# Expert weights of an MoE layer: the later loads as pairs of 4 MiB in a ring of five places

## The chip, the cores and the metric

The kernel runs as one program on one core of a Trainium2 chip. The metric is the time of one execution in microseconds (us); lower is better. TensorE (PE) multiplies matrices, with its weight loads shown as PEld; VectorE (DVE), ScalarE (ACT) and GpSimd (POOL) work on elements; the queue of SyncE (SP) issues nearly all transfers from the memory outside the core (HBM) into the core's SBUF, which has 128 partitions. 16 DMA engines carry those transfers.

## The reference

256 tokens of width 1024 pass through two blocks of attention and feed-forward layers, and then through a second model's block that ends in a mixture of experts. Each token takes the best 4 of 32 experts; only chosen pairs count:

```python
vals, idx = lax.top_k(logits, TOP_K)
gate = jax.nn.softmax(vals, axis=-1)
...
up = jnp.dot(xb, w_up[eb]) + b_up[eb]
glu, lin = jnp.split(up, 2, axis=-1)
glu = jnp.minimum(glu, SWIGLU_LIMIT)
lin = jnp.clip(lin, -SWIGLU_LIMIT, SWIGLU_LIMIT)
act = glu * jax.nn.sigmoid(SWIGLU_ALPHA * glu) * (lin + 1.0)
return jnp.dot(act, w_down[eb]) + b_down[eb]
```

All is float32. The weights of one expert are 1024 x 2048 up and 1024 x 1024 down, 12 MiB; the 32 experts' are 384 MiB, and every expert's weights are read once.

## The kernel before

The first half of the time goes to the attention and feed-forward layers, whose weights come in chunks of 1 MiB (rows of 8 KB, lines 304 and 307). The change doesn't touch them. The MoE layer follows (`moe`).

**Chunks.** On the host, `_expert_chunks` cuts each expert's weights into `PARTS` = 6 chunks of 2 MiB, each [128 partitions x `WIDE` = 4096 floats], so a partition's row is 16 KB. Chunks 0 and 1 hold the gate half of the up weights, 2 and 3 the linear half, 4 and 5 the down weights.

**Units.** The experts are sorted by how many tokens chose them, and take steps of a fixed pattern, `KINDS = "FFFM" + 4 * "MLDLMLL"`. A step of kind L has one unit of 32 token slots, F and M one unit of 64, and D, the busiest experts, two units of 64 slots that use the same six chunks one after the other. For each unit PE runs, in a fixed order, the gate half (chunks 0 and 1), then the down product of the unit before (that one's chunks 4 and 5), then the linear half (chunks 2 and 3). With a D step the chunks 0 and 1 stay in use until its second unit has passed them, which is after the first unit's chunks 2 and 3. All products of tokens and weights are recorded at line 1839 (`products`); the tile of their results is `sc`, the chunks' tile is `ring`. Between the products stand gathers of tokens (line 1804), the outputs' sums (1904) and other small matmuls.

**Loads.** The order of first use makes a list of 192 loads (`seq`), numbered here from 0. D steps after the change's point are the loads 76, 77 (its chunks 0 and 1), 80, 81 (2 and 3), 82, 83 (4 and 5); 118, 119, 122, 123, 124, 125; and 160, 161, 164, 165, 166, 167. Load k goes into place k mod 11 of a ring of `RING` = 11 places, each a pool of one tile of 16 KB in each partition (176 KB in all). The SP queue issues the loads in this order, with line 2019 or 2016. Each issue waits until PE has read the place's old chunk for the last time, and until the transfer issued eight before it has landed, since eight completion semaphores are used in turn. The last chunk comes in three pieces, so that PE can start on it sooner.

```python
t = ring[nd[0] % RING].tile([P, WIDE], F32, tag="ring", name="ring")
...
nc.sync.dma_start(t[:, f], src[bass.ds(row, P), f])
```

After the last unit two places of the ring serve for a row of gains (`post`) and for the result (`res`), and the output leaves in four transfers. `overflow` holds a path for experts with more tokens than their slots, which runs only then.

Of the kernel before, what the change touches and what calls it, by code (L numbers as in the profile page):

```python
# [9 lines left out]
F32 = mybir.dt.float32  # L10
# [9 lines left out]
P = 128  # L20
S = 256
D = 1024
# [11 lines left out]
NE = 32  # L34
# [4 lines left out]
WIDE = 2 * CHUNK  # L39
PARTS = 6  # L40
RING = 11

SLOTS = (0, 8, 1, 6, 7, 5, 2, 9, 10, 3, 4)

WB = (8, 0, 2, 8)
TAKEN = 1000.0
# [86 lines left out]
def _consts2():  # L133
# [26 lines left out]
FIXED = (0, 11, 22)  # L160
# [4 lines left out]
UNITS = [(s, o, n) for s in range(NE)  # L165
         for o, n in {"D": ((0, CAP), (CAP, CAP)), "L": ((0, CAP // 2),)}.get(KINDS[s], ((0, CAP),))]
NU = len(UNITS)
# [37 lines left out]
def _expert_chunks(up, down):  # L205


    u = up.reshape(NE, 2, 4, P, 2, D).transpose(0, 4, 1, 3, 2, 5).reshape(NE, 4, P, WIDE)
    d = down.reshape(NE, 2, 2, 2, P, D).transpose(0, 2, 4, 3, 1, 5).reshape(NE, 2, P, WIDE)
    return np.concatenate([u, d], 1).reshape(NE * PARTS, P, WIDE)  # L210


def _pack(pieces):
# [32 lines left out]
def quads(t):  # L246

    return t.rearrange("p (a b) -> p a b", a=4)
# [86 lines left out]
class Kernel:  # L335
# [1603 lines left out]
    def more_slots(self, ring, positions):  # L1939

        nc, v, tc = self.nc, self.nc.vector, self.tc
        src = self.ins["experts"].rearrange("n p c -> (n p) c")
        with tc.tile_pool(name="ovs", bufs=1) as sp_, tc.tile_pool(name="ovf", bufs=1) as ep:
            at = sp_.tile([P, 1], F32, name="at")
            v.memset(at, 0.0)
            with tc.For_i(0, NE) as e:
                hot = ep.tile([P, NE], F32, tag="hot", name="hot")
                junk = ep.tile([P, NE], F32, tag="junk", name="junk")
                pos = ep.tile([P, 2, 1], F32, tag="opos", name="opos")
                gate = ep.tile([P, 2, 1], F32, tag="ogate", name="ogate")  # L1950
                bsel = ep.tile([96, 1], F32, tag="obsel", name="obsel")
                v.tensor_scalar(hot, self.iota, at, None, ALU.is_equal)
                for t in range(2):
                    for a, b in ((positions, pos), (self.gate, gate)):
                        v.scalar_tensor_tensor(junk, a[:, t], 1.0, hot, ALU.mult, ALU.mult, accum_out=b[:, t])
                v.scalar_tensor_tensor(junk[0:96], self.bsel[0:96], 1.0, hot[0:96], ALU.mult, ALU.mult, accum_out=bsel)
                sel = self.select(bsel, ep)
                for r in range(2):
                    raw = {}

                    def chunk(c):
                        if c not in raw:
                            raw[c] = ring[c].tile([P, WIDE], F32, tag="ring", name="oring")
                            nc.sync.dma_start(raw[c], src[bass.ds((e * PARTS + c) * P, P)])
                        return raw[c]

                    xg = ep.tile([P, KD, CAP], F32, tag="yh", name="oxg")
                    pr = self.pick([(pos[:, :, 0], r * CAP, CAP)])
                    for j in range(0, KD, 2):
                        self.gather(xg, j, pr, self.pt())  # L1970
                    sp, gs = self.spread(pos[:, :, 0], r * CAP, CAP, gate[:, :, 0], ep, 1)
                    gl = self.expert_gate(self.expert_up(0, xg, sel, chunk), ep, "gl", "yl")
                    a = self.expert_turn(self.expert_act(self.expert_up(1, xg, sel, chunk), gl, ep), ep)
                    self.expert_out(self.expert_down(a, sel, gs, chunk, ep, "yh", "yl"), sp)
                v.tensor_scalar(at, at, 1.0, None, ALU.add)

    def moe(self):
        nc, v, tc, ins = self.nc, self.nc.vector, self.tc, self.ins
        ctx = ExitStack()
        ring = [ctx.enter_context(tc.tile_pool(name=f"ring{i}", bufs=1, reuse_waits="tile", side="right"))  # L1980
                for i in range(RING)]
        ring = [ring[i] for i in SLOTS]
        mp = ctx.enter_context(tc.tile_pool(name="moe", bufs=1, reuse_waits="tile"))
        raw, nd = {}, [0]
        src = ins["experts"].rearrange("n p c -> (n p) c")
        which = [None] * NE
# [10 lines left out]
        seq = list(dict.fromkeys(uses))  # L1997
        place = {n: i for i, n in enumerate(seq)}

        spare = [ring[(len(seq) + i) % RING] for i in range(2)]  # L2000

        def load(upto):
            while nd[0] < min(upto, len(seq)):
                e, c = n = seq[nd[0]]
                t = ring[nd[0] % RING].tile([P, WIDE], F32, tag="ring", name="ring")
                row = c * P
                cols = [slice(0, WIDE)]
                if nd[0] == len(seq) - 1:
                    cols = [slice(0, 2 * D), slice(2 * D, 3 * D), slice(3 * D, WIDE)]
                if e >= len(FIXED):  # L2010
                    if which[e] is None:
                        which[e] = nc.values_load(self.order[0:1, e:e + 1], engines=(mybir.EngineType.SP,), min_val=0,
                                                  max_val=NE - 1)
                    row = which[e] * (PARTS * P) + row
                    for f in cols:
                        nc.sync.dma_start(t[:, f], src[bass.ds(row, P), f])
                else:
                    row += FIXED[e] * PARTS * P
                    tc.keep_in_program_order(nc.sync.dma_start(t, src[row:row + P]))
                raw[n] = t  # L2020
                nd[0] += 1

        def chunks(u):
            e = UNITS[u][0]

            def chunk(c):

                load(place[e, c] + (RING if u + 1 == NU or UNITS[u + 1][0] != e else 1))
                return raw[e, c]
            return chunk  # L2030

        load(RING)
        gp = self.gp = ctx.enter_context(tc.tile_pool(name="grp", bufs=1, reuse_waits="tile"))
        groups, spreads = {}, {}
# [26 lines left out]
        def post():  # L2061

            col = self.tiny.tile([P, KD], F32, tag="gcol", name="gcol2", bufs=1)
            v.tensor_tensor(col, self.modc[:, 40:48], self.g2[:, 3], ALU.mult)
            t = spare[0].tile([P, WIDE], F32, tag="ring", name="post")
            self.post_row, r = t[:, 0:D], t[:, D:2 * D].rearrange("p (a b) -> p a b", a=KD)
            v.tensor_tensor(r, self.ones.unsqueeze(1).to_broadcast([P, KD, P]), col.unsqueeze(2).to_broadcast([P, KD, P]),
                            ALU.mult)

            def half(h):  # L2070
                ps = self.pt()
                for i in range(4):
                    nc.tensor.transpose(ps[:, i * P:(i + 1) * P], r[:, 4 * h + i], self.ident)
                nc.scalar.copy(self.post_row[:, h * 512:h * 512 + 512], ps)

            return [lambda h=h: half(h) for h in range(2)]
# [10 lines left out]
        for u, (e, _, _) in enumerate(UNITS):  # L2087
            n = {}
# [39 lines left out]

        def finish():

            res = spare[1].tile([P, WIDE], F32, tag="ring", name="res")[:, 0:2 * D].rearrange("p (t d) -> p t d", t=2)
            s4 = self.tiny.tile([P, 4, 2], F32, tag="ss", name="s4", bufs=1)[:, 0:2]
            half = lambda h: slice(h * 512, h * 512 + 512)
            for t in range(2):
                for h in range(2):
                    nc.scalar.activation(self.sc(), self.out[t][h], AF.Square, accum_out=s4[:, t, h:h + 1])
                for h in (1, 0):
                    v.tensor_tensor(res[:, t, half(h)], self.out[t][h], self.post_row[:, half(h)], ALU.mult)
            r = self.natural_rstd(s4)
            for t in range(2):  # L2140
                for h in range(2):
                    a = res[:, t, half(h)]
                    v.scalar_tensor_tensor(quads(a), quads(a), r[:, t:t + 1], self.x[:, 4 * h:4 * h + 4, t * P:(t + 1) * P],
                                           ALU.mult, ALU.add)
                    nc.sync.dma_start(self.outs["out"][t, :, half(h)], a)

        finish()
        self.overflow([p for p in ring if p not in spare], finish)
        ctx.close()


# [181 lines left out]
```

## Time and profile before

| | us |
|---|---|
| Median of 3 runs | 2136.68 |
| Lowest, highest | 2136.51, 2139.9 |
| The profiled execution: its time | 2137.93 |
| The profiled execution: its span | 2136.2 |
| PE busy in the span | 2010.3 (94%) |
| DVE, ACT busy | 1169.9 (55%), 798.1 (37%) |
| Loads of experts' chunks: 191 of 2048 KB and 3 pieces | 30.4 from issue to landing (median) |

The profile's span runs from the first instruction to the last; the execution's own time is 1.7 us longer. Of the page's 40 slices of 53 us each, those from the 23rd on are the MoE layer.

### The profile page before, as it was taken

The numbers are of one execution on the slowest core, as the hardware profiler recorded it, in microseconds if no ns is written. First come the engines' busy times: TensorE is split into PE (matmuls) and PEld (weight loads), VectorE is DVE, ScalarE is ACT, GpSimd is POOL, SyncE is SP. The second block draws the span as 40 slices with busy tenths as digits, with TensorE's granted clock in tenths as the row PEclk, the third lists the DMA queues.
The fourth block names the chain that finished last, engine by engine and source line by source line (L and its number), as shares of the span: only waits on it lengthen the run. The fifth ranks groups of instructions, "written<-read, shape, count | busy, mean of one in ns | idle before, by whom it ended". The sixth has DMA issues, their size and how long they took to land.

```text
span 2136.2 us, 34339 instructions
## 1 busy us (share of the span) xinstructions
PE 2010.3 (94%) x13872; PEld 1376.2 (64%) x13872; DVE 1169.9 (55%) x2572; ACT 798.1 (37%) x1541; POOL 97.0 (5%) x147
## 2 busy tenths in 40 slices
PE   8999999999999999999999999999789878978895
PEld 6888888888888888888887633444334333433342
DVE  7888878986999887996787522222112111211112
ACT  7655556654554455655576211111101111101111
POOL 1001001221000101000100000000000000000000
PEclk9999999999999999999999999999999999999998
DMA  7555426876765533775535999999999999999996
GB/s 264 200 185 185 156 89 210 303 278 220 251 243 190 196 109 119 258 255 202 187 119 195 391 428 427 406 401 427 428 426 427 427 427 427 426 427 427 428 426 277
DMA packets 66164, 633.89 MB, mean 297 GB/s; under 512 B 10048, under 2 KB 11200, under 8 KB 15312
## 3 DMA queue, kind: packets, MB, share of 16 engines
q1 hardware_dynamic: 59568, 619.62, 73.6%
q0 software_dynamic: 2288, 7.28, 1.0%
q10 hardware_dynamic: 4144, 4.74, 0.7%
q8 instruction: 111, 1.82, 0.3%
q14 instruction: 53, 0.43, 0.1%
HBM read 626.10 MB, written 5.51 MB: 296 GB/s over the span
## 4 chain that ended last, share of the span: by engine, by line
PE 68%; DMA 24%; DVE 5%; ACT 1%; issue 1%; POOL 0%; ACTq 0%; SPq 0%; DVEq 0%; POOLq 0%
DMA ring<-in_experts_dram 22%; PE sc L1839 16%; PE acc L372 14%; PE acc L371 7%; PE sc L372 7%; PE acc L362 4%; PE acc L363 4%; PE acc L364 4%; PE sc L371 3%; DVE wlo L322 1%; PE acc L1904 1%; PE sc L831 1%; PE pv L920 1%; PE pt L1804 1%; PE pv L1804 1%; PE pt L906 1%
## 5 line engine op out<-in xcount | busy, mean ns | idle before, releaser
L1839 PE MATMUL sc<-ring,xg 128*32 128x256 f32 (+1 forms) x3328 | 459.8, 483 | 41.0 <-DMA ring<-in_experts_dram 40.9
L322 DVE TENSOR_TENSOR wlo<-wraw,whi 128x1024 fp32r<-128x1024 f32 (+1 forms) x362 | 441.5, 1223 | 99.4 <-ACT whi L321 97.8
L372 PE MATMUL acc<-xs,whi 128*128 128x512 f32 x1344 | 478.0, 399 | 0.7 <-DVE xs L421 0.4
L321 ACT CAST whi<-wraw 128x1024 fp32r<-128x1024 f32 (+1 forms) x362 | 377.4, 1048 | 258.4 <-PE sc L372 102.3
L371 PE MATMUL acc<-xs,wlo 128*128 128x256 f32 x1344 | 380.9, 284 | 9.5 <-DVE wlo L322 8.2
L372 PEld LDWEIGHTS acc<-xs,whi 128*128 128x128 f32 x1344 | 255.8, 190 | 61.8 <-DVE xs L421 2.3
L1839 PEld LDWEIGHTS sc<-ring,xg 128*32 128x32 f32 (+1 forms) x3328 | 138.9, 122 | 242.8 <-issue 169.8
L371 PEld LDWEIGHTS acc<-xs,wlo 128*128 128x128 f32 x1344 | 254.6, 190 | 11.5 <-DVE wlo L322 9.1
L1839 PE MATMUL sc<-ring,aT 128*32 128x256 f32 (+1 forms) x1664 | 208.8, 480 | 45.7 <-DMA ring<-in_experts_dram 45.6
L372 PE MATMUL sc<-h,whi 128*128 128x512 f32 x704 | 247.6, 394 | 0.0
L371 PE MATMUL sc<-h,wlo 128*128 128x256 f32 x704 | 199.9, 284 | 2.3 <-DVE wlo L322 2.3
L1839 PEld LDWEIGHTS sc<-ring,aT 128*32 128x32 f32 (+1 forms) x1664 | 79.0, 123 | 155.8 <-issue 92.8
L372 PEld LDWEIGHTS sc<-h,whi 128*128 128x128 f32 x704 | 132.3, 188 | 30.2
L1893 DVE SCALAR_TENSOR_TENSOR yl<-sc,gs,yh 128x512 fp32r<-128x512 f32 (+1 forms) x36 | 22.8, 632 | 217.4 <-ACT yh L1892 217.4
L371 PEld LDWEIGHTS sc<-h,wlo 128*128 128x128 f32 x704 | 132.4, 188 | 5.5 <-DVE wlo L322 2.9
L1812 DVE TENSOR_SCALAR xg<-pv,acol,modc 128x128 f32<-128x128 f32 (+2 forms) x58 | 20.6, 397 | 171.1 <-PE pv L1804 171.1
L1821 DVE TENSOR_SCALAR pf<-slots,both 128x128 f32<-128x128 f32 x72 | 17.5, 283 | 176.2 <-PE pv L1824 176.2
L362 PE MATMUL acc<-xs,whi 128*128 128x256 f32 (+1 forms) x368 | 106.3, 289 | 0.0
L364 PE MATMUL acc<-xs,wlo 128*128 128x256 f32 (+1 forms) x368 | 105.3, 286 | 0.0
L363 PE MATMUL acc<-xs,whi 128*128 128x256 f32 (+1 forms) x368 | 104.8, 285 | 0.0
L1892 ACT ACTIVATE yh<-sc,gs 128x512 fp32r<-128x512 f32 (+1 forms) x36 | 21.3, 592 | 223.4 <-PE sc L1839 223.4
L1857 DVE TENSOR_SCALAR gl<-sc 128x512 f32<-128x512 f32 (+1 forms) x36 | 20.6, 573 | 129.4 <-PE sc L1839 129.4
(504 smaller groups left out, 2739.1 us busy)
## 6 DMA issues: line engine op xcount, KB each, us to landing
ring<-in_experts_dram SPq DMA_DIRECT2D x191, 2048.0 KB, 30.4
wraw<-in_weights_dram SPq DMA_DIRECT2D x178, 1024.0 KB, 4.9
wraw<-in_w_ada_dram SPq DMA_DIRECT2D x24, 1024.0 KB, 6.1
skew<-g POOLq DMA_DIRECT2D x8, 264.0 KB, 5.4
wraw<-in_weights_dram SPq DMA_DIRECT2D x4, 512.0 KB, 3.8
bias_dram<-b POOLq DMA_DIRECT2D x8, 208.0 KB, 4.8
w<-skew POOLq DMA_DIRECT2D x8, 200.0 KB, 4.7
bias<-bias_dram ACTq DMA_DIRECT2D x1, 1040.0 KB, 10.8
```

The source lines that it names most:

```text
L321: self.nc.scalar.copy(hi[:, a:b], r[:, o + a:o + b])
L322: self.nc.vector.tensor_tensor(lo[:, a:b], r[:, o + a:o + b], hi[:, a:b], ALU.subtract)
L362: nc.tensor.matmul(out, wh, xh, start=first, stop=False, skip_group_check=True)
L363: nc.tensor.matmul(out, wh, xl, start=False, stop=False, skip_group_check=True)
L364: nc.tensor.matmul(out, wl, xh, start=False, stop=last, skip_group_check=True)
L371: nc.tensor.matmul(ps[:, S:2 * S], wl, x[:, 0], start=first, stop=False, skip_group_check=True)
L372: nc.tensor.matmul(ps, wh, x, start=False, stop=last, skip_group_check=True)
L831: nc.tensor.matmul(o[:, t * S:(t + 1) * S], q[:, t * P:(t + 1) * P], k, start=t == 0, stop=t == 1, skip_group_check=True)
L906: nc.tensor.transpose(ps[:, (kt * 2 + t) * P:(kt * 2 + t + 1) * P], p[:, t, kt * P:(kt + 1) * P], self.ident)
L1804: nc.tensor.matmul(ps[:, i * w:(i + 1) * w], self.x[:, j + i, t * P:(t + 1) * P], pr[:, t], start=t == 0 and i == 0, stop=t == 1, skip_gro ...
L1839: m = self.nc.tensor.matmul(ps[n * h:n * h + n, 0:w], lhs, rhs[:, h * w:h * w + w], start=first, stop=last, skip_group_check=True)
L1893: v.scalar_tensor_tensor(yl, ps, gs, yh, ALU.mult, ALU.subtract)
```

## The change

The two chunks that stand next to each other in use (0 and 1, 2 and 3, 4 and 5) now lie next to each other in HBM: the host's array becomes [384 x 128 x 8192 floats], rows of 32 KB. The loads 0 to 65 still fetch one chunk, half a row of each partition, into the ring of 11. At load 66 (`SWITCH`) that ring is closed and five pools of 32 KB in each partition (160 KB in all) are opened in its space. From there each DMA brings two chunks, 4 MiB with rows of 32 KB, into one place of five; `order` gives out first the places whose old chunks are used up first. There are 63 such pairs; the last comes in four pieces (one chunk, then half a chunk, then two quarters). `post` and `res` take two of the five places, and the overflow path loads pairs.

```diff
-    return np.concatenate([u, d], 1).reshape(NE * PARTS, P, WIDE)
+    w = np.concatenate([u, d], 1).reshape(NE, PARTS // 2, 2, P, WIDE)
+    return w.transpose(0, 1, 3, 2, 4).reshape(NE * PARTS // 2, P, 2 * WIDE)
...
+        order = sorted(range(PAIRS), key=lambda i: max(SLOTS.index(2 * i), SLOTS.index(2 * i + 1)))
...
+                if k == SWITCH:
+                    singles.close()
+                    pools = [ctx.enter_context(tc.tile_pool(name=f"pair{i}", bufs=1, reuse_waits="tile", side="right"))
+                             for i in range(PAIRS)]
+                    pairs.extend(pools[i] for i in order)
...
+                if two:
+                    t = pairs[(k - SWITCH) // 2 % PAIRS].tile([P, 2 * WIDE], F32, tag="ring", name="ring")
+                    cols = [slice(0, 2 * WIDE)]
+                    if k == len(seq) - 2:
+                        cols = [slice(a, b) for a, b in ((0, WIDE), (WIDE, WIDE + 2 * D), (WIDE + 2 * D, WIDE + 3 * D),
+                                                         (WIDE + 3 * D, 2 * WIDE))]
...
-                load(place[e, c] + (RING if u + 1 == NU or UNITS[u + 1][0] != e else 1))
+                k = place[e, c]
+                if u + 1 < NU and UNITS[u + 1][0] == e:
+                    load(k + 1)
+                elif k < SWITCH:
+                    load(min(k + RING, SWITCH))
+                else:
+                    load(k // 2 * 2 + 2 * PAIRS)
                 return raw[e, c]
```

On PE, ACT and POOL no instruction of the path that runs changes its place; on DVE only `post` moves, by two places, in the last unit. What changes is the SP queue, shown at two places. DMAHW0 to DMAHW7 are the eight completion semaphores of transfers, PE the semaphore of TensorE; 128x4096 is one chunk, 128x8192 a pair.

The SP queue around load 66, before: the loads 64 to 69.

```order
L2016 DMA ring<-in_experts_dram 128x4096 [waits DMAHW6_49,PE_49]
L2016 ISA
L2016 DMA ring<-in_experts_dram 128x4096 [waits DMAHW7_49,PE_49]
L2016 ISA
L2016 DMA ring<-in_experts_dram 128x4096 [waits DMAHW0_49,PE_49]
L2016 ISA
L2016 DMA ring<-in_experts_dram 128x4096 [waits DMAHW1_49,PE_49]
L2016 ISA
L2016 DMA ring<-in_experts_dram 128x4096 [waits DMAHW2_49,PE_49]
L2016 ISA
L2016 DMA ring<-in_experts_dram 128x4096 [waits DMAHW3_49,PE_49]
```

The same place with the change: the loads 64 and 65, then the pairs (66, 67), (68, 69), (70, 71) and (72, 73).

```order
L2039 DMA ring<-in_experts_dram 128x4096 [waits DMAHW6_49,PE_49]
L2039 ISA
L2039 DMA ring<-in_experts_dram 128x4096 [waits DMAHW7_49,PE_49]
L2039 ISA
L2039 DMA ring<-in_experts_dram 128x8192 [waits DMAHW0_49,PE_49]
L2039 ISA
L2039 DMA ring<-in_experts_dram 128x8192 [waits DMAHW1_49,PE_49]
L2035 TENSOR_LOAD order
L2035 ISA x2
L2039 ISA
L2039 DMA ring<-in_experts_dram 128x8192 [waits DMAHW4_49,DMAHW2_49,PE_49]
L2039 ISA
```

Each pair waits for PE's last read of the old chunks under both its halves, and only the third and later ones also for a second transfer. Which chunks those are follows from `SLOTS`: for the first five pairs the later one of each is load 57, 59, 62, 64 and 65.

The SP queue at the first D step after the switch, with the change: the pairs (84, 85), (86, 87), (88, 89) and (90, 91).

```order
L2039 DMA ring<-in_experts_dram 128x8192 [waits DMAHW4_49,PE_49]
L2039 ISA
L2039 DMA ring<-in_experts_dram 128x8192 [waits DMAHW5_49,PE_49]
L2035 TENSOR_LOAD order
L2035 ISA x2
L2039 ISA
L2039 DMA ring<-in_experts_dram 128x8192 [waits DMAHW6_49]
L2039 ISA
L2039 DMA ring<-in_experts_dram 128x8192 [waits DMAHW7_49,PE_49]
```

The pair (86, 87) takes the place of the pair (76, 77), the D step's chunks 0 and 1, and waits for PE there; the pair after it, in the place of (78, 79), has no wait for PE of its own, since that pair is used up earlier. Before the change it was load 87 that took the place of load 76, and load 86 went into the place of load 75.

## Rows read from the trace of the kernel before

**Rows 1.** The page: span, and GB/s in its 40 slices.

```profile
span 2136.2 us, 34339 instructions
...
GB/s 264 200 185 185 156 89 210 303 278 220 251 243 190 196 109 119 258 255 202 187 119 195 391 428 427 406 401 427 428 426 427 427 427 427 426 427 427 428 426 277
```

**Rows 2.** Windows: engines, granted clock, DMA share, GB/s; rows of 8 KB, then 16.

```profile
10.00:16.00 6.00, 4.67 (x19) 3.73 (x20) 4.13 (x6) 4.62 (x11) 4.60 (x5) 1.00 1.00 423
...
1500.00:1600.00 100.00, 81.38 (x594) 34.25 (x592) 16.05 (x42) 9.50 (x20) 0.00 (x0) 0.93 1.01 428
```

**Rows 3.** What the SP queue waited for, 1440 to 2120 us: total, times, longest.

```profile
SPq L2016 <- DMA ring<-in_experts_dram: 345.5, 86, 5.9
```

**Rows 4.** The chain that ended last: issue, us to landing, what.

```profile
1452.76 33.80 DMA ring<-in_experts_dram
...
1491.56 39.06 DMA ring<-in_experts_dram
1530.73 40.58 DMA ring<-in_experts_dram
...
1744.27 39.02 DMA ring<-in_experts_dram
...
1951.30 40.56 DMA ring<-in_experts_dram
...
2089.75 30.93 DMA ring<-in_experts_dram
```

**Rows 5.** The tile ring: all its loads, from issue to landing.

```profile
DMA to landing us min/median/max: 7.5/31.0/40.6
```

**Rows 6.** DMA issues by line, from 1133 us to 1530.80, 1744.35 and 1951.40.

```profile
ring<-in_experts_dram SPq DMA_DIRECT2D x81, 2048.0 KB, 17.3
...
ring<-in_experts_dram SPq DMA_DIRECT2D x124, 2048.0 KB, 24.2
...
ring<-in_experts_dram SPq DMA_DIRECT2D x166, 2048.0 KB, 30.2
```

**Rows 7.** Timeline of PE, first D step: start, us, what, [idle before].

```profile
1560.29 1.93 PE L1839 MATMUL sc<-ring,aT 128*32 128x256 f32 x32 [0.90 <-DMA ring<-in_experts_dram]
1566.44 3.64 PE L1839 MATMUL sc<-ring,aT 128*32 128x256 f32 x32 [4.22 <-DMA ring<-in_experts_dram]
1571.45 4.96 PE L1839 MATMUL sc<-ring,xg 128*64 128x512 f32 x12 [1.36 <-DMA ring<-in_experts_dram]
...
1591.55 1.94 PE L1839 MATMUL sc<-ring,xg 128*64 128x512 f32 x8
...
1617.44 7.04 PE L1839 MATMUL sc<-ring,aT 128*64 128x512 f32 x32
```

**Rows 8.** Timeline of PE, second D step.

```profile
1778.53 2.80 PE L1839 MATMUL sc<-ring,xg 128*64 128x512 f32 x12 [1.52 <-DMA ring<-in_experts_dram]
...
1783.33 1.08 PE L1839 MATMUL sc<-ring,xg 128*64 128x512 f32 x4 [0.33 <-DMA ring<-in_experts_dram]
...
1797.03 1.94 PE L1839 MATMUL sc<-ring,xg 128*64 128x512 f32 x8
...
1822.90 7.03 PE L1839 MATMUL sc<-ring,aT 128*64 128x512 f32 x32
```

**Rows 9.** Timeline of PE, third D step.

```profile
1985.74 4.31 PE L1839 MATMUL sc<-ring,xg 128*64 128x512 f32 x12 [2.53 <-DMA ring<-in_experts_dram]
...
1990.66 1.08 PE L1839 MATMUL sc<-ring,xg 128*64 128x512 f32 x4
...
2005.61 1.94 PE L1839 MATMUL sc<-ring,xg 128*64 128x512 f32 x8
...
2031.49 7.04 PE L1839 MATMUL sc<-ring,aT 128*64 128x512 f32 x32
```

**Rows 10.** Windows around the first D step: the granted clock is the third number from the end.

```profile
1565.70:1575.70 10.00, 7.89 (x42) 2.77 (x44) 0.48 (x1) 0.47 (x1) 0.00 (x0) 0.50 1.01 429
1576.00:1600.00 24.00, 24.00 (x132) 9.95 (x132) 4.23 (x10) 2.40 (x5) 0.00 (x0) 1.00 1.01 430
```

More of the change, by code (lines that the diff above doesn't have):

```diff
@@ L43 @@
 SLOTS = (0, 8, 1, 6, 7, 5, 2, 9, 10, 3, 4)
+SWITCH = 66
+PAIRS = RING // 2
 WB = (8, 0, 2, 8)
@@ L1962, in chunk @@
                         if c not in raw:
-                            raw[c] = ring[c].tile([P, WIDE], F32, tag="ring", name="oring")
-                            nc.sync.dma_start(raw[c], src[bass.ds((e * PARTS + c) * P, P)])
+                            t = ring[c // 2].tile([P, 2 * WIDE], F32, tag="ring", name="oring")
+                            nc.sync.dma_start(t, src[bass.ds((e * (PARTS // 2) + c // 2) * P, P)])
+                            for i in range(2):
+                                raw[c // 2 * 2 + i] = t[:, i * WIDE:(i + 1) * WIDE]
                         return raw[c]
@@ L1979, in moe @@
         ctx = ExitStack()
-        ring = [ctx.enter_context(tc.tile_pool(name=f"ring{i}", bufs=1, reuse_waits="tile", side="right"))
+        singles = ExitStack()
+        ring = [singles.enter_context(tc.tile_pool(name=f"ring{i}", bufs=1, reuse_waits="tile", side="right"))
                 for i in range(RING)]
         ring = [ring[i] for i in SLOTS]
+        pairs = []
+        order = sorted(range(PAIRS), key=lambda i: max(SLOTS.index(2 * i), SLOTS.index(2 * i + 1)))
         mp = ctx.enter_context(tc.tile_pool(name="moe", bufs=1, reuse_waits="tile"))
@@ L1998, in moe @@
         place = {n: i for i, n in enumerate(seq)}
-        spare = [ring[(len(seq) + i) % RING] for i in range(2)]
         def load(upto):
             while nd[0] < min(upto, len(seq)):
[L2004 to L2009, printed above, removed]
+                k = nd[0]
+                two = k >= SWITCH
+                if k == SWITCH:
[3 more added lines that the diff above has]
+                    pairs.extend(pools[i] for i in order)
+                e, c = seq[k]
+                row = c // 2 * P
+                if two:
[4 more added lines that the diff above has]
+                                                         (WIDE + 3 * D, 2 * WIDE))]
+                    to, n = t, 2
+                else:
+                    to = ring[k % RING].tile([P, WIDE], F32, tag="ring", name="ring")
+                    o = c % 2 * WIDE
+                    cols = [slice(o, o + WIDE)]
+                    n = 1
                 if e >= len(FIXED):
@@ L2013, in load @@
                                                   max_val=NE - 1)
-                    row = which[e] * (PARTS * P) + row
+                    row = which[e] * (PARTS // 2 * P) + row
                     for f in cols:
-                        nc.sync.dma_start(t[:, f], src[bass.ds(row, P), f])
+                        nc.sync.dma_start(to[:, f] if two else to, src[bass.ds(row, P), f])
                 else:
[L2018 to L2021, printed above, removed]
+                    row += FIXED[e] * (PARTS // 2) * P
+                    tc.keep_in_program_order(nc.sync.dma_start(to, src[row:row + P, cols[0]]))
+                for i in range(n):
+                    raw[seq[k + i]] = to[:, i * WIDE:(i + 1) * WIDE]
+                nd[0] += n
         def chunks(u):
@@ L2026, in chunk, with spare @@
             def chunk(c):
-                load(place[e, c] + (RING if u + 1 == NU or UNITS[u + 1][0] != e else 1))
+                k = place[e, c]
[3 more added lines that the diff above has]
+                    load(min(k + RING, SWITCH))
+                else:
+                    load(k // 2 * 2 + 2 * PAIRS)
                 return raw[e, c]
             return chunk
+        def spare(i):
+            return pairs[((len(seq) - SWITCH) // 2 + i) % PAIRS]
         load(RING)
@@ L2064, in post @@
             v.tensor_tensor(col, self.modc[:, 40:48], self.g2[:, 3], ALU.mult)
-            t = spare[0].tile([P, WIDE], F32, tag="ring", name="post")
+            t = spare(0).tile([P, 2 * WIDE], F32, tag="ring", name="post")
             self.post_row, r = t[:, 0:D], t[:, D:2 * D].rearrange("p (a b) -> p a b", a=KD)
@@ L2129, in finish @@
         def finish():
-            res = spare[1].tile([P, WIDE], F32, tag="ring", name="res")[:, 0:2 * D].rearrange("p (t d) -> p t d", t=2)
+            res = spare(1).tile([P, 2 * WIDE], F32, tag="ring", name="res")[:, 0:2 * D].rearrange("p (t d) -> p t d", t=2)
             s4 = self.tiny.tile([P, 4, 2], F32, tag="ss", name="s4", bufs=1)[:, 0:2]
@@ L2147, in moe @@
         finish()
-        self.overflow([p for p in ring if p not in spare], finish)
+        self.overflow([p for p in pairs if p not in (spare(0), spare(1))], finish)
         ctx.close()
```

## Prediction

> **What bounds the kernel now.** I read the page's slices first, then the windows, the SP queue's waits, the chain, and last the timeline of PE where the chain changes hands. The slices show that from the 23rd on the loads of experts' chunks run at 390 to 428 GB/s until the last slice [rows 1]; the window 1500 to 1600 us has the DMA engines at a share of 1.01 and 428 GB/s while PE is busy 81 us of 100 [rows 2]. So from about 1450 us the end is set by the stream of loads: every microsecond in which the DMA engines have nothing to fetch is added to the time, and PE's waits cost nothing as long as places come free early enough. The SP queue waits mostly for the landing eight loads back, 345.5 us in 86 waits [rows 3], and the chain shows it: a load issued when its eighth predecessor has landed takes 39.06 us, eight loads of 4.9 us [rows 4]. 2 MiB at 428 GB/s are 4.90 us.
>
> The chain leaves the DMA three times after that stretch begins, each time for some 60 us of PE. Load 80 is issued at 1530.73 and lands at 1571.31; load 123 lands at 1744.27 + 39.02 = 1783.29; load 165 at 1951.30 + 40.56 = 1991.86 [rows 4]; the issues counted to these points, 81, 124 and 166, give the numbers [rows 6]. These are the D steps: six chunks serve two units there, so PE needs longer for them than their loads take, and lives on full places. In the first one it is busy for all of 24 us [rows 10]. There the ring's depth decides whether the stream goes on. Before, it does: from the 28th slice to the last but one none shows less than 426 GB/s [rows 1].
>
> A load that finds the engines idle lands 7.5 us after its issue at the least [rows 5], so 7.5 - 4.9 = 2.6 us of it are start and completion. I use this: **a load issued at t leaves a hole of t + 2.6 minus the landing of the load ahead of it**, if that is above zero.
>
> **The rate (gain).** Windows full of 8 KB rows move 423 GB/s, of 16 KB rows 428 [rows 2]: 4.958 and 4.900 us for 2 MiB, so 8 rows fewer on each of the 16 engines are worth 0.058 us. A pair has again 8 rows fewer for each engine than two single loads. 62 pairs (the last of the 63 comes in pieces) x 0.058 = **-3.6 us**; a pair takes 9.74 us. The last digits of the two rates allow 2.9 to 4.3. No row has 32 KB rows, so the ends are wider: 0, if they bring nothing, and 7.2, if the second doubling brings the same 1.2% as the first (62 x 0.116). That longer rows would cost something I leave to a rival, since the one doubling that rows show was a gain. I take 3.6, the same saving for each row.
>
> By the Trainium skill, "DMA: Bandwidth & Descriptors", section "Where 436 GB/s comes from", the ports into SBUF end at 435.2 GB/s; 428 in the rows is under that. A pair could then not take less than 9.64 us (an estimate from that page), a gain of at most 10 us, and the sum below would be 2146.
>
> **The holes (loss).** With five double places two things change in a D step. The place of its chunks 0 and 1 comes free only when both are used up, and the load ahead of the waiting one is one chunk less: load 87 waited for chunk 76 with load 86 still ahead of it; now (86, 87) wait for 76 and 77, with nothing behind load 85. And PE can begin the pair (80, 81) only when both have landed, on one semaphore, so it enters the long stretch later. Step by step:
>
> First D step. Before, PE begins chunk 80 at 1571.45 and reads chunk 77 for the last time at 1591.55 + 1.94 = 1593.49, 22.04 us later [rows 7]. The pair lands at 1571.31 + 4.90 = 1576.21, PE begins at 1576.35, and 77 is free at 1598.4. Load 85 lands at 1571.31 + 5 x 4.90 = 1595.8. Hole: 1598.4 + 2.6 - 1595.8 = 5.2 us. Then (86, 87) land at 1610.7, (88, 89) at 1620.5, (90, 91) at 1630.2; (92, 93) wait for chunk 83, last read before at 1617.44 + 7.04 = 1624.5 [rows 7], now 4.9 later at 1629.4: a hole of 1.8. Together 7.0.
>
> Second. Chunk 123 is the later half of its pair and lands when it did, but PE had done 122 by then, from 1778.53 to 1783.33 - 0.33 = 1783.00 [rows 8], and now does these 4.47 us after the landing. Chunk 119 is free at 1797.03 + 1.94 + 4.47 = 1803.4, load 127 lands at 1783.29 + 4 x 4.90 = 1802.9: a hole of 3.1. Later (134, 135) wait for 125, 1822.90 + 7.03 + 4.47 = 1834.4 [rows 8], and (132, 133) land at 1803.4 + 2.6 + 3 x 9.74 = 1835.2: 1.8. Together 4.9.
>
> Third. Chunk 164 takes from 1985.74 to 1990.66 + 1.08 = 1991.74, 6.0 us that now come after the landing at 1991.86. Chunk 161 is free at 2005.61 + 1.94 + 6.0 = 2013.55 [rows 9], load 169 lands at 2011.5: 4.7. Then (176, 177) wait for 167, 2031.49 + 7.04 + 6.0 = 2044.5 [rows 9], against 2013.55 + 2.6 + 3 x 9.74 = 2045.4: 1.7. Together 6.4.
>
> Sum of the holes: **+18.3 us**. Its bounds come from the clock. After 4.22 us of waiting PE ran chunk 79 in 3.64 us where chunk 78, with the same matmuls, took 1.93 [rows 7], and the granted clock from 1565.7 was 0.50, the lower level of 1.2 GHz [rows 10]. So the first D step was entered slowly: 4.96 us for its first 12 matmuls, 4.31 in the third, 2.80 in the second [rows 7 to 9]. If all three are entered at the full clock, the holes lose 2.2 + 1.5 = 3.7 us (14.6); if the second is entered slowly too, since PE then waits longer, they gain 2.2 (20.5).
>
> **At nothing.** The switch: PE starts on load 63 when it lands at 1452.76 + 33.80 = 1486.56 [rows 4] and has passed all chunks before it, so the places of the first three pairs are free by then, with loads 64 and 65 still to come, 9.8 us of cover against 2.6; were that cover gone, it would be one hole of a few us. Elsewhere in the stream PE waits for pairs, not for halves, but a pair's products fit into its 9.74 us (81% busy), so only their moment moves. The eight-back wait falls away, since five transfers at most are out. SP issues 63 DMAs fewer; its issue times lie under 40 us of queue. `post` waits for load 183 in place of 181, in the last unit, where the loads still to come cover it. The end: the last chunk lands in the same pieces, and from the last landing, 2089.75 + 30.93 = 2120.68 [rows 4], to the end stays 15.5 us of the span of 2136.2.
>
> **Sum.** 18.3 - 3.6 = 14.7. The profiled execution took 2137.93 us: 2152.6. The median of the three runs is 1.25 lower, which would give 2151.4; I say 2152.
>
> **The rivals.**
> *The shift doesn't happen, no holes worth their name* (the other side). If PE got through the D steps as early as now, by running at the full clock and making up for the late start, the holes would be 1593.5 + 2.6 - 1595.8 = 0.3 in the first and none in the others, with some 2 us for the places of chunks 83, 125 and 167: 2.4 - 3.6, 2136.7 us, and with the gain of 7.2 it would be 2133. It decides when the shift is under about 1.3 us instead of 4.5 to 6. For it speaks the half clock on entry; against it that PE was busy for 24.00 of 24 us at the granted clock 1.00 right after [rows 10], so at most 2.2 of 4.9 us can be made up. 7%.
> *Rows of 32 KB are carried as shorter pieces*, so the change in effect doesn't lengthen them: no gain, the holes stay: 2156. 5%.
> *The distance of rows in HBM costs rate.* Partitions' rows now lie 32 KB apart, for the single loads too. From 1486.6 to 2120.7 us the stream sets the time, 634 us, so each per cent of rate is 6.3 us; at 3% 2137.9 + 18.3 + 19 = 2175. No row has loads at such a distance, but 8 and 16 KB differ in the other direction [rows 2]. The Trainium skill, same page, section "Latency and other measured facts", tells that large powers of two between rows slow transfers, 207 GB/s at 512 KiB against 214 in full; that no run here shows, and 32 KB is far below what it lists. 4%.
>
> **The numbers.** My forecast has 84%. About 0.2%, 4.3 us, is what a measurement of this kernel can tell from no change. Faster by more than that needs the first rival with a large gain, 3%; within it 5%; slower 92%. The range: 14.6 - 7.2 gives 2145, less 1 for the median 2144; 20.5 without any gain gives 2158, and 1 more for waits that pairs bring elsewhere: 2144 to 2159. It leaves out most of the first and the third rival.
>
> **What would show it.** Right: GB/s of the slices around 1595, 1810 and 2030 us fall, the SP queue waits for PE there with nothing under way, and the windows between show 430 to 432 GB/s. Each step's hole can be read as the difference between a pair's issue and the landing before it. Wrong: a stream without dips (the first rival), a rate of 428 (the second) or below (the third), or dips elsewhere, above all at the switch near 1496 us.

## The result, and the profile after

The changed kernel takes 2153.93 us (median of 6 runs, 2152.58 to 2155.11) against 2136.65 for the kernel before beside it: a ratio of 1.008, 95% interval 1.007 to 1.009, so some 17 us slower. The forecast was 2152, in a range of 2144 to 2159.

The page of the changed kernel, span and GB/s in 40 slices of 54 us:

```profile
span 2152.5 us, 34097 instructions
...
GB/s 254 200 189 184 155 90 217 298 271 231 242 238 200 192 115 139 253 239 211 198 112 227 400 427 427 405 405 431 430 374 419 433 431 368 419 428 430 370 416 313
```

Up to the 27th slice this is the old profile [rows 1]. Then 431 and 430 stand where 427 and 428 stood, and three slices fall to 374, 368 and 370: those in which the three D steps begin. Windows of the changed kernel (engines, granted clock, DMA share, GB/s):

```profile
1585.00:1605.00 20.00, 20.00 (x104) 7.75 (x101) 4.53 (x10) 2.71 (x5) 0.00 (x0) 1.00 0.70 285
1800.00:1820.00 20.00, 20.00 (x106) 8.13 (x102) 4.40 (x8) 2.71 (x5) 0.00 (x0) 1.00 0.64 260
2014.00:2034.00 20.00, 20.00 (x104) 7.75 (x100) 4.49 (x9) 2.71 (x5) 0.00 (x0) 1.00 0.64 265
...
1575.00:1660.00 85.00, 85.00 (x628) 35.89 (x628) 15.89 (x41) 10.51 (x22) 0.00 (x0) 0.98 0.92 387
1660.00:1789.00 129.00, 95.38 (x868) 44.66 (x865) 20.50 (x60) 11.86 (x26) 0.00 (x0) 0.90 1.01 432
1789.00:1874.00 85.00, 85.00 (x622) 35.53 (x618) 15.87 (x40) 10.51 (x22) 0.00 (x0) 0.98 0.91 382
1874.00:2003.00 129.00, 97.95 (x871) 45.02 (x871) 19.85 (x56) 11.86 (x26) 0.00 (x0) 0.90 1.00 431
2003.00:2088.00 85.00, 85.00 (x619) 35.40 (x616) 14.96 (x36) 10.35 (x22) 0.00 (x0) 0.97 0.90 383
```

In the three D steps PE is busy without a break and the DMA engines are not; between them it is the reverse, at 431 to 432 GB/s. The first three windows, of 20 us, are where the engines stand still most: 6.0, 7.2 and 7.2 us (shares 0.70, 0.64 and 0.64). The kernel before held 427 through the D steps:

```profile
1572.00:1657.00 85.00, 85.00 (x621) 35.44 (x618) 15.86 (x40) 10.52 (x22) 0.00 (x0) 0.98 1.01 427
...
1784.00:1869.00 85.00, 85.00 (x642) 35.98 (x642) 17.60 (x45) 10.93 (x23) 0.00 (x0) 1.00 1.01 427
1992.00:2077.00 85.00, 85.00 (x642) 35.95 (x644) 16.51 (x41) 10.77 (x23) 0.00 (x0) 1.00 1.01 427
```

What the SP queue waited for from 1440 to 2140 us has turned around. Before, the landing eight loads back came first [rows 3]; now it is PE:

```profile
SPq L2039 <- PE sc L1843: 552.3, 61, 43.6
SPq L2039 <- DMA ring<-in_experts_dram: 57.2, 26, 6.5
```

These waits are no loss by themselves: 87.0 us of those for PE lie between 1660 and 1780 us, where the stream runs at 431 GB/s. They cost time only where no transfer is left under way.

The chain of the changed kernel (issue, us to landing) answers to [rows 4]: the pairs (80, 81), (122, 123), (164, 165) and the last piece, with two pairs of the stretch between the first two D steps.

```profile
1533.66 40.26 DMA ring<-in_experts_dram
...
1644.50 34.80 DMA ring<-in_experts_dram
...
1683.66 44.21 DMA ring<-in_experts_dram
...
1746.34 41.16 DMA ring<-in_experts_dram
...
1960.98 40.94 DMA ring<-in_experts_dram
...
2098.75 38.80 DMA ring<-in_experts_dram
```

The landings give an account by stretches. Load 81 came at 1576.2 before and at 1573.9 now, 123 at 1783.3 and 1787.5, 165 at 1991.9 and 2001.9, the last piece at 2120.7 and 2137.6. So the stream is 2.3 us ahead at the first D step, and from there each stretch with one D step loses: 6.5, 5.9 and 6.8 us. The sum, 16.9, is the whole loss within 0.4 us (17.3 by the medians). Of the lead of 2.3 us, 1.6 was there before the switch: PE starts on load 63, a single one in both kernels, at 1485.01 us in the changed kernel's profiled execution and at 1486.60 in the other. The rows of 1644.50 and 1683.66 give the rate: the landings at 1679.30 and 1727.87 are five pairs apart, 9.715 us each. Before, nine loads landed from 1486.56 to 1530.62 [rows 4], 9.79 us for two.

The entry to the D steps on PE, in the changed kernel (start, us, what, [idle before]); answers to [rows 7 to 9]:

```profile
1563.04 3.66 PE L1843 MATMUL sc<-ring,aT 128*32 128x256 f32 x64 [0.92 <-DMA ring<-in_experts_dram]
1574.06 4.67 PE L1843 MATMUL sc<-ring,xg 128*64 128x512 f32 x12 [7.35 <-DMA ring<-in_experts_dram]
...
1593.89 1.94 PE L1843 MATMUL sc<-ring,xg 128*64 128x512 f32 x8
```

```profile
1787.64 5.39 PE L1843 MATMUL sc<-ring,xg 128*64 128x512 f32 x12 [7.41 <-DMA ring<-in_experts_dram]
```

```profile
2002.05 5.39 PE L1843 MATMUL sc<-ring,xg 128*64 128x512 f32 x12 [6.06 <-DMA ring<-in_experts_dram]
...
2002.00:2007.40 5.40, 5.35 (x14) 1.42 (x14) 0.00 (x0) 0.00 (x0) 0.00 (x0) 0.50 1.04 446
```

PE now does both chunks ahead of the step at once (64 matmuls), waits 6 to 7 us for the pair and begins at the lower clock: the granted clock was 0.50 from 2002.0 to 2007.4 us (the last row, a window), 0.51 in the same part of the second D step and 0.61 in the first. Chunk 77 is free at 1593.89 + 1.94 = 1595.83, and the SP queue's timeline has the issue of (86, 87) at 1595.87, the first row here; the first issues of the same kind in the other two steps follow:

```profile
1595.87 1.47 SPq L2039 DMA_DIRECT2D ring<-in_experts_dram  x2
...
1810.17 0.33 SPq L2039 DMA_DIRECT2D ring<-in_experts_dram  x1
...
2024.83 0.33 SPq L2039 DMA_DIRECT2D ring<-in_experts_dram  x1
```

The pair (84, 85), two after (80, 81), was down by about 1573.9 + 2 x 9.72 = 1593.4. The rule of the prediction makes 1595.87 + 2.6 - 1593.4 = 5.1 us of hole of it.

### The profile page after: what moved, and what is told of

Read it like the earlier page. It is cut to its first block, busy times and chain, and to the rows that moved or that the text cites. A ratio compares the mean times of both kernels' runs of the same rounds, so it can differ in the third digit from the quotient of the medians.

```text
span 2152.5 us, 34097 instructions
## 1 busy us (share of the span) xinstructions
PE 2019.0 (94%) x13872; PEld 1384.2 (64%) x13872; DVE 1169.5 (54%) x2572; ACT 798.4 (37%) x1541; POOL 99.6 (5%) x147
## 4 chain that ended last, share of the span: by engine, by line
PE 74%; DMA 18%; DVE 5%; ACT 1%; issue 1%; POOL 0%; ACTq 0%; SPq 0%; DVEq 0%; POOLq 0%
PE sc L1843 21%; DMA ring<-in_experts_dram 17%; PE acc L376 14%; PE acc L375 7%; PE sc L376 7%; PE acc L366 4%; PE acc L367 4%; PE acc L368 4%; PE sc L375 3%; PE acc L1908 2%; DVE wlo L326 1%; PE sc L835 1%; PE pv L1808 1%; PE pt L1808 1%; PE pv L924 1%; PE pt L910 1%
## 5 line engine op out<-in xcount | busy, mean ns | idle before, releaser
L1843 PE MATMUL sc<-ring,xg 128*32 128x256 f32 (+1 forms) x3328 | 469.7, 492 | 70.9 <-DMA ring<-in_experts_dram 69.7
```

The source lines that it names most:

```text
L1843: m = self.nc.tensor.matmul(ps[n * h:n * h + n, 0:w], lhs, rhs[:, h * w:h * w + w], start=first, stop=last, skip_group_check=True)
```

## The experiments

The theory was that the loss needs two things at once: PE enters a D step late, because it must wait for both chunks of a pair, and the ring has one chunk less and so no reserve for that. (The runs bear out the first half; what they say of the second stands with late_ten.) The rivals put it down to the arrangement in HBM, to the places that come free in pairs, to the missing place alone, or to the late entry alone. All times below are medians, with the ratio to the kernel before run beside them (2136.17 us for ten_single, all_halves and mixed_ring, 2135.58 for the other four). The name in brackets is used further on.

**The arrangement alone.** (layout_alone) All loads single, in the ring of eleven, from rows that lie 32 KB apart.

```diff
-                row = c * P
+                row = c // 2 * P
+                o = c % 2 * WIDE
...
-                        nc.sync.dma_start(t[:, f], src[bass.ds(row, P), f])
+                        nc.sync.dma_start(t[:, f], src[bass.ds(row, P), slice(o + f.start, o + f.stop)])
```

> The kernel before with only the new arrangement in HBM: all 192 loads single with rows of 16 KB that lie 32 KB apart, ring of eleven places. Theory (the loss is holes in the stream of loads at the D steps, which need the ring of five and the late entry): no change, 2135.5 to 2138. Rival (distance of rows in HBM costs rate): slower, 6.3 us for each per cent of rate; the 17 us lost by the change would need 2.7%, so about 2154.

Measured: 2136.19 us, ratio 1.0003 (0.9994 to 1.0012). Its GB/s in the slices are the old ones:

```profile
GB/s 256 197 195 183 158 90 204 294 275 223 253 251 177 213 109 119 255 257 200 191 119 189 391 428 427 410 399 428 426 429 426 426 427 427 428 426 427 427 427 277
```

The distance of 32 KB costs nothing that can be measured; this rival is out.

**Three pairs of 63 split.** (split_three) The changed kernel, with only the D steps' chunks 2 and 3 fetched by two DMAs into the same double place.

```diff
                     cols = [slice(0, 2 * WIDE)]
+                    if k in (80, 122, 164):
+                        cols = [slice(0, WIDE), slice(WIDE, 2 * WIDE)]
```

> The changed kernel, with 3 of its 63 pairs, those of the D steps' chunks 2 and 3 (loads 80 and 81, 122 and 123, 164 and 165), fetched by two DMAs of one chunk each into the same double place, so that PE can begin the first half when it has landed. Places, their release and all other pairs stay. Theory (the late entry of PE makes the holes, on top of a ring that has just no reserve left): holes of 5 to 6 us shrink to about 0.5, the later ones of about 1.5 stay in part, the rate's gain stays: 2134 to 2138, no change against the kernel before, 16 to 18 us under the changed kernel. Rival (the loss comes from double places that come free late, whatever PE does): 2150 to 2154.

Measured: 2136.0 us, ratio 1.0002 (0.9993 to 1.0011). Three split transfers take back the whole loss. Timeline of PE at the first D step, then the windows at the three:

```profile
1567.54 2.80 PE L1843 MATMUL sc<-ring,xg 128*64 128x512 f32 x12 [2.78 <-DMA ring<-in_experts_dram]
...
1572.35 1.08 PE L1843 MATMUL sc<-ring,xg 128*64 128x512 f32 x4 [0.34 <-DMA ring<-in_experts_dram]
...
1570.00:1655.00 85.00, 84.67 (x644) 35.93 (x644) 17.61 (x45) 10.94 (x23) 0.00 (x0) 1.00 0.99 418
1780.00:1865.00 85.00, 85.00 (x642) 35.85 (x640) 17.61 (x45) 10.94 (x23) 0.00 (x0) 1.00 1.00 421
1990.00:2075.00 85.00, 85.00 (x640) 36.01 (x634) 16.51 (x41) 10.78 (x23) 0.00 (x0) 1.00 0.99 417
```

PE starts on chunk 80 when it lands, waits 0.34 us for 81 as before the change, and does its first 12 matmuls in 2.80 us. The D steps run at 417 to 421 GB/s in place of 382 to 387. They are still under 427, by 9, 6 and 10 GB/s, which is 5.0 us in the three windows: the places in pairs cost that, and the longer rows of the other pairs (59 x 0.075 = 4.4 us) pay for it. The pairs' release by itself is not the whole cause; that PE must wait for the whole pair is needed too. PE also enters the D step at the full clock here, so what the split gives back holds the lower clock's cost as well.

**Late entry with eleven places.** (late_eleven) The kernel before, with the order of two loads exchanged in each D step.

```diff
         seq = list(dict.fromkeys(uses))
+        for i in (80, 122, 164):
+            seq[i:i + 2] = seq[i + 1], seq[i]
...
```

> The kernel before, single loads and eleven places, with the loads of chunks 2 and 3 of the three D steps exchanged in order, so that PE, which wants chunk 2 first, enters each D step 4.5 to 6 us later, as with a pair. Theory: with eleven places there is reserve for it (load 87 is issued about 12 us before load 86 lands), so nothing happens: 2136 to 2138. Rival (a late entry of PE alone costs its 5 us at each of three D steps): 2150 to 2153.

Measured: 2137.96 us, ratio 1.0011 (1.0002 to 1.002): 2.4 us above the run beside it, at the upper end of what was expected (the rival: 15). The entry was indeed late, at the first D step:

```profile
1575.56 5.39 PE L1839 MATMUL sc<-ring,xg 128*64 128x512 f32 x12 [6.24 <-DMA ring<-in_experts_dram]
```

All the same the engines have work there while the loads into the places of chunks 0 and 1 go out (DMA share 1.01 from 1585 to 1605 us); the little that is lost comes after that (0.91 from 1605 to 1625 us).

**Ten places alone.** (ten_single) The kernel before, with ten single places from load 66 on.

```diff
-                t = ring[nd[0] % RING].tile([P, WIDE], F32, tag="ring", name="ring")
+                t = ring[nd[0] % RING if nd[0] < 66 else (nd[0] - 66) % 10].tile([P, WIDE], F32, tag="ring", name="ring")
...
```

> The kernel before with a ring of ten single places from load 66 on, loads in their own order. Theory (a place less costs nothing as long as PE enters the D steps on time): 2135 to 2138, the same as before. Rival (the missing place by itself makes the holes): 2146 to 2151, as with the late entry.

Measured: 2136.64 us, ratio 1.0 (0.9991 to 1.0009). A place less, by itself, costs nothing that can be measured as long as the places are single.

**Late entry with ten places.** (late_ten) Both edits together, still with single loads of 16 KB rows.

> The same exchange, and from load 66 on a ring of ten single places in place of eleven (each chunk's place comes free by itself). Theory: the late entry and the missing place together make holes even without pairs, 4 to 5 us at the first and third D step and 2 to 3 at the second: 2146 to 2151. Rival (only places that come free in pairs make holes): 2136 to 2139.

Measured: 2151.32 us, ratio 1.0072 (1.0057 to 1.0088), 0.3 us above what was expected. By ratio the four cases are: neither 1, a place less 1.0000, the exchange 1.0011, both 1.0072. The two edits cost next to nothing apart and 15 us together. But the loss doesn't lie where the changed kernel has it. Windows of 20 us: the first three hold the loads into the places of a D step's chunks 0 and 1, the next three those into the places of chunks 2 and 3; the last three are the changed kernel's, for chunks 2 and 3.

```profile
1585.00:1605.00 20.00, 20.00 (x106) 8.24 (x104) 4.07 (x8) 2.86 (x6) 0.00 (x0) 1.00 0.97 388
1797.00:1817.00 20.00, 20.00 (x103) 7.98 (x104) 4.52 (x11) 3.09 (x6) 0.00 (x0) 1.00 0.91 365
2010.00:2030.00 20.00, 20.00 (x103) 7.76 (x102) 4.75 (x11) 3.09 (x6) 0.00 (x0) 1.00 0.97 389
...
1605.00:1625.00 20.00, 20.00 (x152) 8.14 (x150) 4.66 (x14) 2.50 (x6) 0.00 (x0) 1.00 0.84 336
1820.00:1840.00 20.00, 20.00 (x162) 8.17 (x162) 4.66 (x14) 2.17 (x5) 0.00 (x0) 1.00 0.82 336
2033.00:2053.00 20.00, 20.00 (x164) 8.32 (x166) 3.77 (x10) 2.41 (x5) 0.00 (x0) 1.00 0.81 329
...
1605.00:1625.00 20.00, 20.00 (x156) 8.72 (x157) 4.66 (x14) 2.64 (x6) 0.00 (x0) 1.00 1.00 430
1820.00:1840.00 20.00, 20.00 (x153) 8.23 (x153) 4.66 (x14) 2.65 (x6) 0.00 (x0) 1.00 1.01 433
2034.00:2054.00 20.00, 20.00 (x156) 8.73 (x157) 3.77 (x10) 2.64 (x6) 0.00 (x0) 1.00 0.99 427
```

The changed kernel stood still for 6.0, 7.2 and 7.2 us at the places of chunks 0 and 1 and not at all at those of 2 and 3. Here it is 0.6, 1.8 and 0.6 us, and then 3.2, 3.6 and 3.8. The exchange does more than delay PE: the place that is next in the ring now holds chunk 3, which is used up after chunk 2. In the first D step load 90 waits for chunk 3's last read, 1612.76 + 1.08 = 1613.84 (PE, then the SP queue):

```profile
1612.76 1.08 PE L1839 MATMUL sc<-ring,xg 128*64 128x512 f32 x4
...
1589.33 0.33 SPq L2019 DMA_DIRECT2D ring<-in_experts_dram  x1
...
1594.74 2.25 SPq L2019 DMA_DIRECT2D ring<-in_experts_dram  x3
...
1613.88 0.87 SPq L2019 DMA_DIRECT2D ring<-in_experts_dram  x2
```

In the kernel before, the loads into the places of chunks 2 and 3 were issued at 1606.32 and 1612.66 us, 6.3 apart; without that wait load 90 would have been early enough, as the engines stood still for 3.2 us there. So this run doesn't show that a late entry and a missing place make the changed kernel's loss, and it can't rule out places that come free in pairs, since the exchange imitates just that for chunks 2 and 3. The SP rows tell how much such a release weighs: load 86, into the place of chunk 76, goes at 1589.33 us, and load 87, into that of chunk 77, at 1594.74. A pair would have had to wait for both, 5.4 us longer, and that is about the hole that the changed kernel has there.

**Every pair in two halves.** (all_halves) The changed kernel's double places, filled by two DMAs each.

```diff
-                    cols = [slice(0, 2 * WIDE)]
+                    cols = [slice(0, WIDE), slice(WIDE, 2 * WIDE)]
```

> The changed kernel with every pair fetched by two DMAs of one chunk each (rows of 16 KB) into its double place: the ring of five double places without the long rows and without the late entry. Theory: the rate's gain of 4 to 5 us is gone, holes of about 0.5 and 1.6 us at the D steps stay: 2137 to 2140. It stands above split_three by the rate's gain. Rival (double places are the cause): 2152 to 2156.

Measured: 2142.1 us, ratio 1.0024 (1.0014 to 1.0034): 2 us above what was expected, far below the rival. This is the ring of five double places without the late entry, and it costs 5 to 6 us: less than the change, but not nothing. Against split_three it is 0.22% or 4.7 us slower, which fits the longer rows' part of 4.4 us. Its D steps run at 408 to 417 GB/s:

```profile
1570.00:1655.00 85.00, 83.02 (x622) 34.65 (x616) 16.34 (x41) 10.93 (x23) 0.00 (x0) 1.00 0.99 417
1780.00:1865.00 85.00, 84.45 (x612) 35.12 (x616) 16.17 (x41) 10.25 (x22) 0.00 (x0) 0.97 0.97 408
1990.00:2075.00 85.00, 82.99 (x620) 34.64 (x616) 15.44 (x37) 10.82 (x23) 0.00 (x0) 1.00 0.99 412
```

Against 427 that is 8.8 us in the three windows, but this profiled execution took 2145.11 us, 3 us above the median. Holes of 0.5 and 1.6 us at each of three D steps add up to 6.3 us, so the holes expected fit what was measured better than the range of 2137 to 2140 did.

**Pairs except at the D steps.** (mixed_ring) From load 66 on five double places, but for the twelve loads of each D step eleven single ones, opened and closed in the same space. They are laid out so that after the step the single places that come free one after the other are neighbours and make a double place.

```diff
+MIXED = (66, 76, 88, 118, 130, 160, 172, 192)
+DPLACES = (0, 2, 10, 1, 3, 4, 6, 8, 5, 7, 9, 10)
...
+                two = k >= SWITCH and MIXED.index(max(m for m in MIXED if m <= k)) % 2 == 0
+                if k in MIXED:
+                    singles.close() if k == SWITCH else phase[0].close()
+                    phase[0] = ExitStack()
...
+                        d_pools[:] = [pools[2 * where[i // 2] + i % 2] if i < 10 else pools[10] for i in DPLACES]
```

> A version meant to beat both: pairs of 4 MiB in five double places except for the twelve loads at each D step (76 to 87, 118 to 129, 160 to 171), which go singly into eleven places, so laid out that after the step the places that come free next to each other in time lie next to each other. 45 pairs in place of 63. Theory: no holes, a gain of 44 times 0.075 us in rate (a pair landed 9.715 us after the one before it in the changed kernel, two single loads 9.79): 3.3 us under the kernel before, 2132 to 2134 when that is at 2135.6 to 2136.7. Rival (the rate's gain is lost elsewhere, at the changes of ring): the same as before or slower.

Measured: 2132.63 us, ratio 0.9985 (0.9976 to 0.9994): faster than both kernels, by 3.2 us and some 21 us. From the 28th on its slices keep 425 to 432 GB/s until the last one, and 44 of its loads are pairs (the 45th comes in pieces); page and DMA issues:

```profile
GB/s 262 199 189 184 158 90 205 304 271 221 253 252 177 212 110 119 257 257 201 191 119 191 391 428 427 412 396 429 428 427 432 431 427 430 431 431 425 431 430 272
...
ring<-in_experts_dram SPq DMA_DIRECT2D x44, 4096.0 KB, 33.3
```

So the longer rows do bring what the rate said, about 0.07 us for each pair (3.2 / 44), once nothing starves the stream.

## Why the prediction was right

**What bounds it** held: the stream of loads sets the end, and the loss is time in which the DMA engines had nothing to fetch, at the three D steps and nowhere else. The switch at load 66 made no hole; the slices there read 431 and 430.

**The holes** were in the right places by the right steps. In the first D step chunk 77 came free 21.8 us after PE began the pair (1574.06 to 1595.83), the step said 22.0, and the rule gives a first hole of 5.1 against 5.2. In the other two steps the pair ahead was down 19.43 us after 1787.5 and 2001.9, and the rule gives 1810.17 + 2.6 - 1806.9 = 5.9 and 2024.83 + 2.6 - 2021.3 = 6.1, against 3.1 and 4.7. What was sized too low is the sum: the stretches lost 6.5, 5.9 and 6.8 us net of the rate's gain. With 0.075 us back for each of the 21, 21 and 12 pairs in them the holes are 8.1, 7.4 and 7.7, 23.2 us in place of 18.3. Of the 4.9 us that are missing, 4.2 are these two first holes, and the rows for them are there: the first 12 matmuls took 5.39 us in both, not the 2.80 of [rows 8] and the 4.31 of [rows 9], because PE had now waited 7.41 and 6.06 us and began at the lower clock. The bound of the clock term foresaw the second step's part (2.2 us; it was 2.6) and not the third's (1.1). The remaining 0.7 or so, in the later holes, was not taken apart.

**The rate** was sized too low as well: 3.6 us, where 62 x 0.075 makes 4.6. That it came so close is partly luck. The 423 GB/s for rows of 8 KB stand on one window of 6 us, and the same window of the changed kernel, over the same rows of 8 KB, reads 430:

```profile
10.00:16.00 6.00, 4.08 (x16) 3.27 (x16) 4.10 (x6) 4.63 (x11) 4.55 (x5) 0.88 1.02 430
```

From that reading the same working would have found no gain in longer rows at all. The gain itself is real, as mixed_ring shows; its size was not in the rows that it was taken from. The two errors have opposite signs, and the lead of 1.6 us from before the switch takes some more away (23.2 - 4.6 - 1.6 = 17.0), which is why 14.7 against the measured 17 looks better than its terms do.

**The rivals.** That PE would make up for the late entry is refuted by the entries themselves, which got slower and not faster; its point of decision was sound, as split_three shows, where the shift is gone and with it the loss. Its price was not: it put the holes without the shift at 2.4 us, and all_halves lost 5 to 6. Rows cut into shorter pieces: 431 and 432 GB/s speak against it, and so do the packets of the whole execution, before and after:

```profile
DMA packets 66164, 633.89 MB, mean 297 GB/s; under 512 B 10048, under 2 KB 11200, under 8 KB 15312
...
DMA packets 57235, 633.87 MB, mean 294 GB/s; under 512 B 9057, under 2 KB 10209, under 8 KB 14321
```

8929 fewer packets for the same bytes are 144 for each of 62 pairs: 128 rows and 16 small packets (991 fewer under 512 B). So a row of 32 KB goes as one packet. The distance in HBM: layout_alone. By the Trainium skill, "DMA: Bandwidth & Descriptors", section "Where 436 GB/s comes from", the ports end at 435.2 GB/s; the windows of 129 us here show up to 432 and one slice of the page 433. So, by that page, the longer rows come close to the ceiling and leave little for still longer ones.

**What the prediction did not say** is what its two causes do one by one. It added them in one sum. The late entry with eleven single places costs 2.4 us (late_eleven), five double places without it 5 to 6 (all_halves), and the two together some 22 before the rate's gain (17.3 + 4.6). So most of the sum only stands for both together: the pair that must wait for chunk 77 as well, and PE that comes late to chunk 77. What part the eleventh place has in it stays open. Single places show no loss without it (ten_single), late_ten has its holes elsewhere, and no run has double places with room for eleven chunks.

## What to carry to other kernels

A larger transfer changes three things apart from its rate: the place is held until its last part is read, the first part can't be read before the last has landed, and the ring has fewer steps of reserve. Here the first cost 5 to 6 us alone and the second, with single places, 2.4, but both together some 22. Find the stretch in which the consumer is slower than the stream and lives on the ring, and work out there when the next place comes free against when the queue runs dry; the average busy shares don't show it. If the reserve is gone only in a few places, go back to small transfers there alone: three transfers of 63 were enough to undo the loss, and twelve at each such place gave a gain.

## What was not expected of the hardware

Windows of 129 us with rows of 32 KB held 431 and 432 GB/s, against 427 for 16 KB in windows of 85 us: about 1% for the doubling, where half as much had been expected. What rows of 8 KB hold at a full queue these runs don't settle: the window from 10 to 16 us reads 423 in the kernel before and 430 in the changed one.

A longer wait of PE had its price later. In the changed kernel all three D steps were entered at the lower clock after waits of 6.06 to 7.41 us, 4.67 to 5.39 us for 12 matmuls; with three pairs split all three were entered at 2.79 or 2.80 us after waits of 2.78, 2.77 and 1.24. The last wait alone doesn't decide it: in mixed_ring the second D step was entered at 4.49 us after 2.55, and in the kernel before the first at 4.96 after 1.36 [rows 7]. The lower clock costs time here because PE is on the chain from its entry into a D step on.
